# A decoder step in float32: head norms by matmul, query norm in the scores, weights split per 128 columns

## The chip, the cores and the metric

The kernel runs on one core of a Trainium2 chip. The metric is device time in microseconds (us), the median of several executions; a profiled execution gives the trace. The engines are TensorE (PE, matmuls; PEld its weight loads), VectorE (DVE), ScalarE (ACT), GpSimd (POOL) and SyncE (SP, which issues most DMAs). TensorE's granted clock is given as a share of 2.4 GHz.

## The reference

One step of a decoder layer for a prompt of 1024 tokens and 64 sample tokens (8 sequences of 8), model width 1024, feed-forward width 2816, in float32:

```
x += 0.5 * swiglu_1(rms(x))
h  = rms(x);  q | k | v | u | g_a | g_b = h @ w_in
q, k = head_rms(q) * q_norm, head_rms(k) * k_norm        # 12 heads of 64, each head normalised by itself
A  = dilated window attention, 3 groups of 4 heads: (window, dilation) = (128,1), (512,4), (2048,16)
     logits = q.k / 8 + bias[distance];  groups combined per position by their softmax denominators
B  = causal means of u over 2/4/8/16 positions minus the token, linear map per group, scale
x += (sigmoid(g_a) * (A @ w_attn) + sigmoid(g_b) * (B @ w_pool)) @ w_out
x += 0.5 * swiglu_2(rms(x))
head_rms(y) = y * rsqrt(mean over the head's 64 of y*y + 1e-6)
```

The normalised keys and the values of the last window, the sample tokens' new cache rows and the pooling state are outputs too.

## The kernel before

Activations lie feature-major (features on the 128 partitions, tokens along the free dimension), in three chunks of 360, 360 and 368 tokens. Every float32 product is three matmuls of split operands: ScalarE copies the operand into the high part (`split`, L212), VectorE subtracts it for the low part (L213), and `mm3` multiplies high by high (L257), low by high (L258) and high by low (L259). A projection (`proj`) of 128 columns for one chunk is 24 matmuls into one PSUM tile `psa`. Weights are loaded and split in units of 256 columns (`wr` loaded, `wh` and `wl` split, two units at a time).

The stages in order: loads, transposes and first norm; FFN 1 (11 blocks j: gate, up, and `down` of the block before); the second norm (`norm` sums squares by matmul with ones, L305, builds a diagonal `dg` of roots, spreads it by a matmul, L322, multiplies, L325, and splits into `h_hi`, L328, and `h_lo`, L329, of which every third on GpSimd) beside the U projections (L535); then for the groups 2, 1 and 0 in turn projections of q, k and v, with the attention of the group before and the sample scores emitted between them; gates, combination, merge, output projection (L1181), a third norm, FFN 2.

The order of instructions on each engine is fixed when the program is built: jobs are generators that an interleaver advances by a modelled clock (`il.spawn`, `yield` of a delay, `go`), and each engine works through its own list in order.

Head norms (`qk_norm`) run per pair of token tiles: transposes to token-major (L710), squares on ScalarE (L736), a sum per head on VectorE (L739), eleven small operations for the root (L741, L280 to L287), product with the root (L744), for keys the gain on GpSimd (L749), the stores, transposes back (L766; for queries with a flipped identity), copies (L771, L774). Attention of a tile (`attention`): scores (L799), bias added on VectorE (L802), maximum (L805), exp (L808), transposes (L817), values (L831), the result stored by a DMA on GpSimd's queue (L834). Sample scores (`sample_scores`): cached keys `kt` and queries `qb` loaded by SyncE, multiplied (L856) and summed (L858) on VectorE. At the start, `biases` multiplies the bias table out (L428) and stores it (`f_scr`), from which 13 small DMAs and more on GpSimd's queue build the sample tokens' bias (`b_scr`, L490, L493).

Of the kernel before, what the change touches and what calls it, by code (L numbers as in the profile page):

```python
# [11 lines left out]
F32 = mybir.dt.float32  # L12
F32R = mybir.dt.float32r
# [30 lines left out]
FD = (4, 3)  # L44
# [73 lines left out]
def body(ctx, tc, x_prompt, x_sample, c128, c512, c2048, state_pool, rel_bias_table,  # L118
         norm_ffn1, ffn1_w_up, ffn1_w_down, norm_mix, w_in, q_norm, k_norm, pool_w_group,
         pool_scale, w_attn_branch, w_pool_branch, w_out, norm_ffn2, ffn2_w_up, ffn2_w_down,  # L120
         onehots, hmask, flipped, y_prompt, y_sample, kvp0, kvp1, kvp2, pool_p, kvs0, kvs1, kvs2, pool_s):
# [11 lines left out]
    wp = ctx.enter_context(tc.tile_pool(name="wp", bufs=2))  # L133
# [17 lines left out]
    flip = const.tile([P, P], F32, name="flip")  # L151
    G.dma_start(out=flip, in_=flipped)
# [8 lines left out]
    gq = const.tile([P, 2, 3], F32, name="gq")  # L161
# [19 lines left out]
    f_scr = dr.tile([4, 4, BL], F32, name="f_scr")  # L181

# [32 lines left out]
    def wunit(src, k, n):  # L215
        wh = wp.tile([P, k, n], F32R, tag="wh", name="wh")
        wl = wp.tile([P, k, n], F32R, tag="wl", name="wl")
        hk = max(k // 2, 1)
        for k0 in range(0, k, hk):
            raw = wp.tile([P, hk, n], F32, tag="wr", name="wr", bufs=3)  # L220
            load(raw, src[k0 * P:(k0 + hk) * P].rearrange("(k p) n -> p k n", p=P))
            split(wh[:, k0:k0 + hk, :], wl[:, k0:k0 + hk, :], raw)
        return wh, wl
# [3 lines left out]
    def fetch(*srcs):  # L227

        wh = wp.tile([P, KD, 256], F32R, tag="wh", name="wh")
        wl = wp.tile([P, KD, 256], F32R, tag="wl", name="wl")  # L230

        def steps():
            raws, k = [], 0
            for src in srcs:
                for r in range(0, src.shape[0], 512):
                    m = min(src.shape[0] - r, 512) // P
                    raw = wp.tile([P, 4, 256], F32, tag="wr", name="wr", bufs=3)[:, :m]
                    load(raw, src[r:r + m * P].rearrange("(k p) n -> p k n", p=P))
                    raws.append((raw, slice(k, k + m)))
                    k += m  # L240
            for i, (raw, sl) in enumerate(raws):
                yield FD[i]
                split(wh[:, sl, :], wl[:, sl, :], raw)

        fetched.append(((wh, wl), il.spawn(steps())))
# [15 lines left out]
    def proj(w, half, c, hi, lo, ks=(0, KD)):  # L261
# [4 lines left out]
        sl = slice(half * P, half * P + P)  # L266
        mm3(o, [(w[0][:, k, sl], w[1][:, k, sl], hi[:, k, c0:c0 + n], lo[:, k, c0:c0 + n])
# [64 lines left out]
    def ffn(xt, w_up, w_down, ncopy, hook):  # L332
# [52 lines left out]
        for j in range(11):  # L385
            wg = wunit(w_up[:, j * 256:(j + 1) * 256], KD, 256)
# [6 lines left out]
            wu = wunit(w_up[:, DFF + j * 256:DFF + (j + 1) * 256], KD, 256)  # L393
# [26 lines left out]
    def biases():  # L420
# [4 lines left out]
        for g in range(4):  # L425
# [5 lines left out]
            G.dma_start(out=f_scr[g], in_=fr)  # L431

# [96 lines left out]
    wus = [wunit(wi[:, OFF_U + i * 256:OFF_U + (i + 1) * 256], KD, 256) for i in range(2)]  # L529
    for c in range(3):  # L530
        c0, n = CH[c]
        for gi in range(4):
# [66 lines left out]
    def permute(g, dst, o, c):  # L599
# [3 lines left out]
        if g == 0:  # L603
            S.activation(dst[:, c0:c0 + n], o, AF.Copy)
            return
        if g == 2:
            S.activation(dst[:, :TP].rearrange("p (r i) -> p r i", r=8)[:, :, c0 // 8:(c0 + m) // 8],
                         o[:, :m].rearrange("p (i r) -> p r i", r=8), AF.Copy)
        else:
            dv = dst[:, :TP].rearrange("p (r f i) -> p r f i", r=4, f=2)  # L610
            for hf in range(2):
                a, b = max(c0, 512 * hf), min(c0 + m, 512 * hf + 512)
                if a < b:
                    S.activation(dv[:, :, hf, (a - 512 * hf) // 4:(b - 512 * hf) // 4],
                                 o[:, a - c0:b - c0].rearrange("p (i r) -> p r i", r=4), AF.Copy)
        if m < n:
            S.activation(dst[:, TP:], o[:, m:n], AF.Copy)
# [9 lines left out]

    def reversed_rows(dst, g, t):

        if g == 0:  # L630
            return dst[(7 - t) * P:(8 - t) * P]
        if g == 1:
            r = 515 - 512 * (t % 2) - t // 2
            return dst[r:r + 509:4]
        return dst[7 - t:7 - t + 1017:8]
# [17 lines left out]
    def qkv(g, gp, follow):  # L653
# [3 lines left out]
        jobs = []  # L657
        qs = qp.tile([P, 2, NS], F32, tag="qs", name="qs", bufs=1)
        ks = qp.tile([P, 2, NS], F32, tag="ks", name="ks", bufs=1)
        for kind in range(3):  # L660
            c0 = kind * AW + g * 256
            w = taken()
            raw = [rp.tile([P, T], F32, tag="raw", name="raw") for _ in range(2)]
            gt = None
            if kind < 2:
                gt = qp.tile([P, 256], F32, tag="gt", name="gt", bufs=1)
                src = (q_norm, k_norm)[kind]
                G.dma_start(out=gt, in_=bass.AP(tensor=src.tensor, offset=src.offset + g * 256,
                                                ap=[[0, P], [1, 256]]))
                if kind == 0:  # L670
                    V.tensor_scalar(out=gt, in0=gt, scalar1=0.125, scalar2=None, op0=ALU.mult)
            for f in range(2):
                for c in range(3):
# [3 lines left out]
                    permute(g, raw[f], o, c)  # L677
                    go()
            for u in range(5):
                tiles = (2 * u, 2 * u + 1) if u < 4 else (8,)  # L680
                jobs.append(il.spawn(
                    values_of(g, tiles, raw, vs) if kind == 2 else
                    qk_norm(g, kind, tiles, raw, gt, qT if kind == 0 else kT,
                            qs if kind == 0 else ks), 1.5 + 2 * u))

        def new_scores():
            for i in range(2):
# [5 lines left out]
                V.tensor_copy(s_new[:, g, i::2, :], o.rearrange("p (h k) -> p h k", h=2))  # L693
# [3 lines left out]
        def tail():  # L697
            for job in jobs:
                il.finish(job)
            yield from new_scores()  # L700

        return qT, kT, vs, il.spawn(tail(), 11)

    def token_major(raw, tiles):
# [3 lines left out]
        for i, t in enumerate(tiles):  # L708
            for a in range(2):
                PE.transpose(out=o[:rows, i * 256 + a * P:i * 256 + (a + 1) * P],  # L710
                             in_=raw[a][:, t * P:t * P + rows], identity=ident)
        return o[:rows, :len(tiles) * 256]

    def values_of(g, tiles, raw, vs):
        o = token_major(raw, tiles)
        il.clock += 0.22 * len(tiles)
        if len(tiles) == 1:
            vt = xq()[:, :256]
            S.activation(vt[:NS], o, AF.Copy)
            store_kv(g, 8, 1, vt)  # L720
            return
        S.activation(vs[:, tiles[0]:tiles[0] + 2, :], o.rearrange("p (t f) -> p t f", f=256), AF.Copy)
        for t in tiles:
            store_kv(g, t, 1, vs[:, t, :])
        return
        yield

    def qk_norm(g, kind, tiles, raw, gt, dst, dst8):
        nt = len(tiles)
        n = nt * 256  # L730
        nh = nt * 4
        o = token_major(raw, tiles)
        rows = o.shape[0]
        il.clock += 0.22 * nt
        sq = xq()[:rows]
        S.activation(sq[:, :n], o, AF.Square)  # L736
        st = qp.tile([P, 3, 8], F32, tag="st", name="st", bufs=3)
# [531 lines left out]
```

## Time and profile before

| | |
|---|---|
| median of 3 runs | 2480.33 us (2477.65 to 2481.48) |
| profiled execution: its time | 2478.45 us |
| its span, first to last instruction | 2476.7 us |
| mean granted clock of TensorE | 0.979 |
| busy: TensorE, VectorE, ScalarE, GpSimd | 2400.4, 1151.3, 604.0, 203.2 us |

The time is 1.75 us longer than the span. Busy time counts an instruction that runs at the lower clock with its full, longer duration, and counts matmuls that overlap in the pipeline once.

### The profile page before, as it was taken

The numbers are of one execution on the slowest core, as the hardware profiler recorded it, in microseconds if no ns is written. First come the engines' busy times: TensorE is split into PE (matmuls) and PEld (weight loads), VectorE is DVE, ScalarE is ACT, GpSimd is POOL, SyncE is SP. The second block draws the span as 40 slices with busy tenths as digits, with TensorE's granted clock in tenths as the row PEclk, the third lists the DMA queues.
The fourth block names the chain that finished last, engine by engine and source line by source line (L and its number), as shares of the span: only waits on it lengthen the run. The fifth ranks groups of instructions, "written<-read, shape, count | busy, mean of one in ns | idle before, by whom it ended". The sixth has DMA issues, their size and how long they took to land.

```text
span 2476.7 us, 35593 instructions
## 1 busy us (share of the span) xinstructions
PE 2400.4 (97%) x14706; PEld 2344.0 (95%) x14706; DVE 1151.3 (46%) x2451; ACT 604.0 (24%) x1293; POOL 203.2 (8%) x317
## 2 busy tenths in 40 slices
PE   7999999999999999979779999999999999999999
PEld 6999999999999999968679889999999999999998
DVE  6333433333344855766768425646333333443334
ACT  5211111111112433423323222223111111111111
POOL 4200000000000303111121110011000000000001
PEclk8999999999999999979889999999999999999999
DMA  4311212122120224455545773712121221222132
GB/s 143 106 51 51 85 68 85 35 85 85 68 85 27 93 74 133 153 177 185 169 134 171 253 254 123 254 52 68 69 69 52 85 85 69 86 69 85 31 114 73
DMA packets 153586, 257.17 MB, mean 104 GB/s; under 512 B 12580, under 2 KB 122852, under 8 KB 152640
## 3 DMA queue, kind: packets, MB, share of 16 engines
q1 hardware_dynamic: 141296, 224.26, 27.8%
q0 software_dynamic: 12128, 30.64, 3.7%
q8 instruction: 115, 1.88, 0.3%
q14 instruction: 47, 0.39, 0.1%
HBM read 225.99 MB, written 73.57 MB: 121 GB/s over the span
## 4 chain that ended last, share of the span: by engine, by line
PE 85%; issue 5%; DMA 4%; DVE 4%; POOL 1%; ACT 0%; SPq 0%; DVEq 0%; POOLq 0%
PE psa L258 21%; PE psa L257 20%; PE psa L259 20%; PE psb L258 7%; PE psb L257 7%; PE psb L259 7%; DMA qb<-q_scr 3%; DVE qb L856 1%; DVE sc L858 1%; DMA u_scr<-us 1%; PE psb L1017 1%; DMA wr<-in_ffn_w_up_dram 1%; PE psb L831 0%; POOL xq L749 0%; PE psa L1213 0%
## 5 line engine op out<-in xcount | busy, mean ns | idle before, releaser
L257 PE MATMUL psa<-h_hi,wh 128*128 128x360 f32 (+1 forms) x3216 | 1064.5, 331 | 4.5 <-ACT h_hi L328 2.0
L258 PE MATMUL psa<-h_lo,wh 128*128 128x360 f32 (+1 forms) x3216 | 1064.2, 331 | 1.9 <-DVE h_lo L329 1.9
L259 PE MATMUL psa<-h_hi,wl 128*128 128x360 f32 (+1 forms) x3216 | 1061.3, 330 | 0.0
L257 PEld LDWEIGHTS psa<-h_hi,wh 128*128 128x128 f32 x3216 | 609.4, 190 | 12.0 <-ACT h_hi L328 2.7
L258 PEld LDWEIGHTS psa<-h_lo,wh 128*128 128x128 f32 x3216 | 609.5, 190 | 6.4 <-issue 2.9
L259 PEld LDWEIGHTS psa<-h_hi,wl 128*128 128x128 f32 x3216 | 609.0, 189 | 6.4 <-issue 5.2
L357 DVE SCALAR_TENSOR_TENSOR xt<-psb,xt 128x360 f32<-128x360 f32 (+1 forms) x528 | 279.8, 533 | 624.5 <-PE psb L259 624.2
L257 PE MATMUL psb<-hh,dh 128*128 128x360 f32 (+1 forms) x1056 | 347.2, 329 | 0.0
L258 PE MATMUL psb<-hl,dh 128*128 128x360 f32 (+1 forms) x1056 | 346.8, 328 | 0.0
L259 PE MATMUL psb<-hh,dl 128*128 128x360 f32 (+1 forms) x1056 | 346.2, 328 | 0.0
L257 PEld LDWEIGHTS psb<-hh,dh 128*128 128x128 f32 x1056 | 198.6, 188 | 0.2
L258 PEld LDWEIGHTS psb<-hl,dh 128*128 128x128 f32 x1056 | 198.5, 188 | 0.1
L259 PEld LDWEIGHTS psb<-hh,dl 128*128 128x128 f32 x1056 | 198.4, 188 | 0.0
L213 DVE TENSOR_TENSOR wl<-wr,wh 128x1024 fp32r<-128x1024 f32 (+1 forms) x142 | 167.7, 1204 | 61.5 <-ACT wh L212 61.4
L212 ACT ACTIVATE dh<-dr 128x256 fp32r<-128x256 f32 x176 | 72.3, 417 | 493.4 <-PE psb L258 482.4
L212 ACT ACTIVATE wh<-wr 128x1024 fp32r<-128x1024 f32 (+1 forms) x142 | 141.1, 1040 | 180.6 <-PE psa L258 180.3
L380 DVE TENSOR_TENSOR tmp<-tmp,psa 128x360 f32<-128x360 f32 x132 | 70.0, 530 | 217.2 <-PE psa L259 217.2
L373 ACT ACTIVATE tmp<-psa 128x360 f32<-128x360 f32 x132 | 62.1, 470 | 330.4 <-PE psa L259 329.9
L212 ACT ACTIVATE hh<-tmp 128x360 fp32r<-128x360 f32 x132 | 66.2, 502 | 271.2 <-DVE tmp L380 269.0
L213 DVE TENSOR_TENSOR dl<-dr,dh 128x256 fp32r<-128x256 f32 x176 | 73.0, 421 | 48.1 <-ACT dh L212 48.1
L213 DVE TENSOR_TENSOR hl<-tmp,hh 128x360 fp32r<-128x360 f32 x132 | 70.2, 534 | 48.3 <-ACT hh L212 48.1
L856 DVE TENSOR_TENSOR qb<-kt,qb 128x512 f32<-128x512 f32 x96 | 67.3, 702 | 43.9 <-DMA qb<-q_scr 43.8
(227 smaller groups left out, 1601.3 us busy)
## 6 DMA issues: line engine op xcount, KB each, us to landing
wr<-in_ffn_w_up_dram SPq DMA_DIRECT2D x88, 512.0 KB, 4.3
out_dram<-in_cache_kv_w_dram SPq DMA_DIRECT2D x32, 1020.0 KB, 9.0
qb<-q_scr SPq DMA_DIRECT2D x96, 256.0 KB, 3.9
dr<-in_ffn_w_down_dram SPq DMA_DIRECT2D x44, 512.0 KB, 4.2
wr<-in_w_in_dram SPq DMA_DIRECT2D x38, 512.0 KB, 4.8
kt<-in_cache_kv_w_dram SPq DMA_DIRECT2D x64, 256.0 KB, 3.3
vt<-in_cache_kv_w_dram SPq DMA_DIRECT2D x26, 512.0 KB, 7.9
t<-t_scr SPq DMA_DIRECT2D x16, 544.0 KB, 4.8
```

The source lines that it names most:

```text
L212: S.activation(hi, src, AF.Copy)
L213: V.tensor_tensor(out=lo, in0=src, in1=hi.bitcast(F32), op=ALU.subtract)
L257: PE.matmul(out, lh, rh, start=i == 0, stop=False)
L258: PE.matmul(out, lh, rl, start=False, stop=False)
L259: PE.matmul(out, ll, rh, start=False, stop=i == n - 1)
L357: V.scalar_tensor_tensor(out=xd, in0=o, scalar=0.5, in1=xd, op0=ALU.mult, op1=ALU.add)
L373: S.activation(t, o, AF.Silu)
L380: V.tensor_tensor(out=t, in0=t, in1=o, op=ALU.mult)
L856: V.tensor_tensor(out=qb, in0=kt.to_broadcast([P, 2, 256]) if g == 0 else kt, in1=qb, op=ALU.mult))
L858: V.tensor_reduce(out=sc[g][:, t0 * 4:t0 * 4 + 8], in_=qb.rearrange("p a (h d) -> p (a h) d", d=64), axis=AX.X, op=ALU.add)
L1017: PE.matmul(o[32 * i:32 * i + 32, :], pz[g][:, 4 * j + i, r], vt[:, i, :], start=False, stop=g == 2 and r == 7)
```

## The change

Squares of q and k come straight from the projections' PSUM on ScalarE (`sqs`); `head_norms` sums them per head by 18 matmuls with a two-column matrix `halves`, and makes all roots of a projection in one chain on tiles of 36 columns. Queries are not normalised in place: they are written with their gain to `qT`, and the root `rq` multiplies the scores, in one operation per head with the bias. Only the 64 sample queries are normalised as tokens (`queries`). Keys get their gain on the way out of PSUM and the root in token-major form (`keys`); their transposes back (`back`) come one tile pair later. The bias table is stored a second time, once per partition (`f_rep`). Weights are held in half units of 128 columns, three at a time, and loops over chunks run inside loops over 128-column halves in block 0 of the FFNs, the U projections and the last unit of the output projection. Four `kt` and `qb` buffers in place of three, four `raw` buffers in place of three; tokens are no longer flipped in `u_scr`.

```diff
+FD = (4, 3, 3, 2)
-    wp = ctx.enter_context(tc.tile_pool(name="wp", bufs=2))
+    wp = ctx.enter_context(tc.tile_pool(name="wp", bufs=3))
+    def wtiles():
+        return [[wp.tile([P, KD, P], F32R, tag=x, name=x) for x in ("wh", "wl")] for _ in range(2)]
+    def wsplit(w, f, sl, raw):
+        split(w[f][0][:, sl, :], w[f][1][:, sl, :], raw[:, :, f * P:(f + 1) * P])
...
             if prev is None:
-                for c in range(3):
-                    for f in range(2):
-                        sil[f, c] = gate(wg, f, c)
-                    for f in range(2):
-                        up(wu, f, c, sil[f, c], hh, hl)
+                for f in range(2):
+                    for c in range(3):
+                        up(wu, f, c, gate(wg, f, c), hh, hl)
...
             G.dma_start(out=f_scr[g], in_=fr)
+            if g != 2:
+                G.dma_start(out=f_rep[g], in_=fr.unsqueeze(1).to_broadcast([4, P, BL]))
...
-    for c in range(3):
-        c0, n = CH[c]
-        for gi in range(4):
+    for c, gi in [(c, gi) for i in range(2) for c in range(3) for gi in (2 * i, 2 * i + 1)]:
+            c0, n = CH[c]
...
+                    if kind == 0:
+                        permute(g, qT[:, f], qs[:, f], o, c, scale=gq[:, 0, f, g:g + 1])
+                    else:
+                        permute(g, raws[f][:, :TP], raws[f][:, TP:], o, c,
+                                scale=gq[:, 1, f, g:g + 1] if kind == 1 else 1.0)
+                    if kind < 2:
+                        permute(g, sqs[f][:, :TP], sqs[f][:, TP:], o, c, AF.Square)
...
+    def head_norms(sqs, y):
+        o = psb()
+        for t in range(9):
+            rows = P if t < 8 else NS
+            for f in range(2):
+                PE.matmul(o[:rows, 4 * t + 2 * f:4 * t + 2 * f + 2], sqs[f][:, t * P:t * P + rows],
+                          halves, start=True, stop=True)
...
+        for rows, cols in ((P, slice(0, 32)), (NS, slice(32, 36))):
+            V.tensor_scalar(out=v[:rows, cols], in0=o[:rows, cols], scalar1=1.0 / 64, scalar2=EPS,
+                            op0=ALU.mult, op1=ALU.add)
         rsqrt(v, y, t_)
...
-        if kind == 1 or nt == 1:
-            G.tensor_tensor(out=xv, in0=xv, in1=gt[:rows].unsqueeze(1).to_broadcast([rows, nt, 256]),
-                            op=ALU.mult)
...
+            pending.append((tiles, xn))
+            yield 1.8
+            if len(pending) > 1:
+                back(*pending.pop(0))
...
-                V.tensor_tensor(out=s[:, i::2, :], in0=o.rearrange("p (a k) -> p a k", a=2),
-                                in1=bias[:, i::2, nb - nk:], op=ALU.add)
+                for a in range(2):
+                    h = 2 * a + i
+                    V.scalar_tensor_tensor(out=s[:, h, :], in0=o[:, a * nk:(a + 1) * nk],
+                                           scalar=rq[:, 4 * t + h:4 * t + h + 1],
+                                           in1=bias[:, h, nb - nk:], op0=ALU.mult, op1=ALU.add)
...
-                    if len(loaded) > 2:
+                    if len(loaded) > 3:
                         multiply(*loaded.pop(0))
...
-    for c in range(3):
-        for d in range(4, 8):
-            out_proj(wos[d // 2 - 2], d % 2, d, c)
-        pend[c] = il.spawn(norm(xt, c, 2))
+        for f, c in [(f, c) for f in range(2) for c in range(3)] if i < 3 else \
+                [(f, c) for c in range(3) for f in range(2)]:
...
+            if i == 3 and f:
+                pend[c] = il.spawn(norm(xt, c, 2))
```

TensorE, keys of the middle group (1), before: its list where the attention of group 2 ends. `raw` is the projected key, `xq` the normalised one, `s` and `pt` the scores and their transposes, `vs` the values.

```order
L831 MATMUL psb<-vs,pt 128x64 x4
L799 MATMUL psb<-kT,qT 128x128 x4
L817 MATMUL psb<-ident,s 128x128 x4
L831 MATMUL psb<-vs,pt 128x64 x4
L817 MATMUL psb<-ident,s 128x128 x4
L831 MATMUL psb<-vs,pt 128x64 x4
L710 MATMUL psb<-ident,raw 128x128 x16
L766 MATMUL psb<-ident,xq 128x128 x4
L710 MATMUL psb<-ident,raw 64x128 x2
```

The same place now: the sums of squares, two tile pairs of transposes and the first projection matmuls behind them.

```order
L730 MATMUL psb<-halves,sqs 128x2 x16
L730 MATMUL psb<-halves,sqs 64x2 x2
L717 MATMUL psb<-ident,raw 128x128 x8
L269 MATMUL psa<-h_hi,wh 128x360
L270 MATMUL psa<-h_lo,wh 128x360
L271 MATMUL psa<-h_hi,wl 128x360
```

Before, the back-transposes (L766) of the first pair follow the transposes (L710) directly; now 31 projection matmuls, of which three are shown, stand before the first back-transposes (L770), and 23 to 27 between the later ones.

VectorE at the keys of group 2, now (`st` and `rk` hold the roots, `qb` the sample queries, `xq` the normalised keys; before, each pair of tiles had its own such chain of 128x8 operations between the sample products, L856 and L858).

```order
L297 SCALAR_TENSOR_TENSOR st<-rk 128x36
L298 TENSOR_TENSOR st<-st 128x36
L299 SCALAR_TENSOR_TENSOR rk<-st,rk 128x36
L889 TENSOR_TENSOR qb<-kt,qb 128x512
L781 TENSOR_TENSOR xq<-psb,rk 128x512 x2
L889 TENSOR_TENSOR qb<-kt,qb 128x512
L891 TENSOR_REDUCE sc_7665<-qb 128x8
```

The chain ends with L299, and the products of keys and roots (L781) then stand among sample products (L889) and their sums (L891).

TensorE in the U projections, now, where chunk 1 (360 columns, `psa_7420`) ends and chunk 2 (368 columns) begins; L334 spreads chunk 2's roots, `psa_7500` is the second unit's first half on chunk 0.

```order
L270 MATMUL psa_7420<-h_lo_92,wh_7223 128x360
L334 MATMUL psb_7382<-tmp_7343,ones_78 128x368
L271 MATMUL psa_7420<-h_hi_91,wl_7224 128x360
L269 MATMUL psa_7420<-h_hi_91,wh_7223 128x360
L270 MATMUL psa_7420<-h_lo_92,wh_7223 128x360
L271 MATMUL psa_7420<-h_hi_91,wl_7224 128x360
L562 MATMUL psb_7742<-ident_69,xq_7218 128x120 x4
L269 MATMUL psa_7446<-h_hi_91,wh_7221 128x368
L269 MATMUL psa_7473<-h_hi_91,wh_7223 128x368
L269 MATMUL psa_7500<-h_hi_91,wh_7297 128x360
```

Before, four projections of each chunk stood ahead of the next chunk's diagonal; now two do, and the first matmuls of chunk 2's tiles stand ahead of the 24 on `psa_7500`.

GpSimd at the start, now: the bias table's stores and the last low halves of chunk 2 (368 columns).

```order
L443 DMA f_rep<-fr 512x1x448
L341 TENSOR_TENSOR h_lo<-tmp,h_hi 128x368
L502 DMA b_scr<-f_scr 8x4x128 x8
L505 DMA b_scr<-f_scr 32x1x8 x4
L341 TENSOR_TENSOR h_lo<-tmp,h_hi 128x368
L441 DMA f_scr<-fr 4x448
L443 DMA f_rep<-fr 512x1x448
```

Before, the list was the same without `f_rep` (and with five of the small DMAs in place of four ahead of the last low half).

## Rows read from the trace of the kernel before

**Rows 1.** The page's first part: busy us (share of the span) and instructions of each engine.

```profile
PE 2400.4 (97%) x14706; PEld 2344.0 (95%) x14706; DVE 1151.3 (46%) x2451; ACT 604.0 (24%) x1293; POOL 203.2 (8%) x317
```

**Rows 2.** Stretches: length, busy PE PEld DVE ACT POOL, clock, DMA share, GB/s.

```profile
60.00:800.00 740.00, 740.00 (x4481) 740.00 (x4481) 270.42 (x501) 139.22 (x260) 17.53 (x32) 1.00 0.21 69
...
1060.00:1140.00 80.00, 60.45 (x344) 55.13 (x344) 51.98 (x134) 21.46 (x58) 17.26 (x23) 0.81 0.63 196
1140.00:1220.00 80.00, 71.24 (x450) 64.32 (x449) 56.81 (x139) 33.52 (x100) 6.84 (x11) 0.91 0.49 152
1220.00:1280.00 60.00, 35.01 (x195) 31.36 (x194) 43.54 (x116) 10.21 (x22) 12.68 (x14) 0.72 0.50 161
1280.00:1345.00 65.00, 63.67 (x424) 59.49 (x423) 50.13 (x106) 28.33 (x89) 9.82 (x18) 0.97 0.55 176
1640.00:1712.00 72.00, 72.00 (x438) 71.31 (x437) 49.97 (x116) 27.08 (x54) 15.31 (x15) 1.00 0.10 30
```

**Rows 3.** Waits of TensorE, 1000 to 1345 us: total, times, longest.

```profile
PE psb L766 <- POOL xq L749: 35.1, 6, 12.1
```

**Rows 4.** Timeline of TensorE: start, length, instruction, in brackets idle time before it.

```profile
1234.00 1.12 PE L766 MATMUL psb<-ident,xq 128*128 128x128 f32 x4 [9.34 <-POOL xq L749]
...
1237.26 0.50 PE L258 MATMUL psa<-h_lo,wh 128*128 128x360 f32 x1
1237.56 0.50 PE L259 MATMUL psa<-h_hi,wl 128*128 128x360 f32 x1
...
1244.26 0.60 PE L766 MATMUL psb<-ident,xq 128*128 128x128 f32 x4
```

**Rows 5.** A group of TensorE, 1000 to 1340 us: busy us, mean ns, idle before.

```profile
L257 PE MATMUL psa<-h_hi,wh 128*128 128x360 f32 x227 | 79.3, 349 | 2.1 <-ACT xq L1135 1.0 <-ACT raw L604 0.7 <-ACT raw L614 0.3
```

**Rows 6.** Timeline of VectorE, 1228 to 1272 us.

```profile
1240.02 0.69 DVE L856 TENSOR_TENSOR qb<-kt,qb 128x512 f32<-128x512 f32 x1 [1.90 <-DMA qb<-q_scr]
...
1241.35 0.68 DVE L744 TENSOR_TENSOR xq<-psb,st 128x512 f32<-128x512 f32 x1
...
1242.66 0.77 DVE L741 TENSOR_SCALAR st<-st 128x8 f32<-128x8 f32 x1
```

**Rows 7.** Timeline of GpSimd, 1225 to 1280 us.

```profile
1242.11 1.29 POOL L749 TENSOR_TENSOR xq<-xq,gt 128x512 f32<-128x512 f32 x1 [8.16 <-DVE xq L744]
```

**Rows 8.** Groups of VectorE, 1000 to 1340 us, forms kept apart.

```profile
L856 DVE TENSOR_TENSOR qb<-kt,qb 128x512 f32<-128x512 f32 x83 | 57.3, 691 | 39.4 <-DMA qb<-q_scr 39.3
...
L802 DVE TENSOR_TENSOR s<-psb,bias 128x512 f32<-128x512 f32 x20 | 13.2, 683 | 5.4 <-PE psb L799 5.4
...
L802 DVE TENSOR_TENSOR s<-psb,bias 128x256 f32<-128x256 f32 x22 | 8.6, 416 | 10.7 <-PE psb L799 10.6
L285 DVE SCALAR_TENSOR_TENSOR st<-st 128x8 f32<-128x8 f32 x48 | 7.9, 166 | 1.4
```

**Rows 9.** Timeline of TensorE, 808 to 866 us: second norm.

```profile
812.08 0.72 PE L305 MATMUL psb<-ones,tmp 128*128 128x1 f32 x6
...
824.69 0.43 PE L258 MATMUL psa<-h_lo,wh 128*128 128x360 f32 x1 [1.87 <-DVE h_lo L329]
```

**Rows 10.** Timeline of VectorE, 815 to 862 us.

```profile
838.47 2.09 DVE L325 SCALAR_TENSOR_TENSOR tmp<-xt,gains,psb 128x360 f32<-128x360 f32 x4
...
858.32 3.60 DVE L329 TENSOR_TENSOR h_lo<-tmp,h_hi 128x368 fp32r<-128x368 f32 x5
```

**Rows 11.** Timeline of TensorE, 1640 to 1712 us: third norm.

```profile
1648.58 0.72 PE L305 MATMUL psb<-ones,tmp 128*128 128x1 f32 x6
...
1671.12 0.72 PE L305 MATMUL psb<-ones,tmp 128*128 128x1 f32 x6
```

**Rows 12.** Timeline of GpSimd, 25 to 75 us.

```profile
59.73 1.02 POOL L329 TENSOR_TENSOR h_lo<-tmp,h_hi 128x368 fp32r<-128x368 f32 x1
```

**Rows 13.** Timeline of TensorE: the first matmul of chunk 2.

```profile
69.77 0.33 PE L257 MATMUL psa<-h_hi,wh 128*128 128x368 f32 x1
```

**Rows 14.** The page's groups: busy us, mean ns, idle before.

```profile
L213 DVE TENSOR_TENSOR wl<-wr,wh 128x1024 fp32r<-128x1024 f32 (+1 forms) x142 | 167.7, 1204 | 61.5 <-ACT wh L212 61.4
```

More of the change, by code (lines that the diff above doesn't have):

```diff
@@ L43 @@
 SPACE = 2.7
-FD = (4, 3)
+FD = (4, 3, 3, 2)
 CDELAY = 12
@@ L150, in body @@
     make_identity(nc, ident)
-    flip = const.tile([P, P], F32, name="flip")
-    G.dma_start(out=flip, in_=flipped)
+    halves = const.tile([P, 2], F32, name="halves")
+    V.memset(halves, 0.0)
+    for i in range(2):
+        V.memset(halves[64 * i:64 * i + 64, i:i + 1], 1.0)
     ones = const.tile([P, P], F32, name="ones")
@@ L240, in steps @@
                     k += m
[L241 to L245, printed above, removed]
+            for f in range(2):
+                for i, (raw, sl) in enumerate(raws):
+                    yield FD[2 * f + i]
+                    wsplit(w, f, sl, raw)
+        fetched.append((w, il.spawn(steps())))
     def taken():
@@ L662, in qkv @@
             w = taken()
[L663 to L671, printed above, removed]
+            raws, sqs = [], []
             for f in range(2):
+                if kind:
+                    raws.append(rp.tile([P, T], F32, tag="raw", name="raw"))
+                if kind < 2:
+                    sqs.append(rp.tile([P, T], F32, tag="raw", name="sqs"))
                 for c in range(3):
@@ L711, in token_major @@
                              in_=raw[a][:, t * P:t * P + rows], identity=ident)
+        il.clock += 0.22 * len(tiles)
         return o[:rows, :len(tiles) * 256]
[L714 to L726, printed above, removed]
@@ new lines, in by_head, with queries @@
+    def by_head(y, tiles, rows):
+        c = slice(4 * tiles[0], 4 * tiles[-1] + 4)
+        return y[:rows, c].unsqueeze(2).to_broadcast([rows, 4 * len(tiles), 64])
+    def queries(g, sqs, rq, qs):
+        head_norms(sqs, rq)
+        yield 5
+        o = psb()
+        for a in range(2):
+            PE.transpose(out=o[:NS, a * P:(a + 1) * P], in_=qs[:, a, :], identity=ident)
+        xn = xq()[:NS, :256]
+        V.tensor_tensor(out=xn.rearrange("p (h d) -> p h d", d=64),
+                        in0=o[:NS, :256].rearrange("p (h d) -> p h d", d=64),
+                        in1=by_head(rq, (8,), NS), op=ALU.mult)
+        G.dma_start(out=q_scr[g], in_=xn)
+        q_ready[g] = True
@@ new lines, in keys, with back @@
+    def keys(g, raws, sqs, kT, ks):
+        rk = qp.tile([P, 36], F32, tag="rk", name="rk", bufs=1)
+        head_norms(sqs, rk)
+        yield 4
+        pending = []
+        def back(tiles, xn):
+            nt, rows = len(tiles), xn.shape[0]
+            tr = psb()
+            for i in range(nt):
+                for a in range(2):
+                    PE.transpose(out=tr[:, (a * nt + i) * rows:(a * nt + i + 1) * rows],
+                                 in_=xn[:, i * 256 + a * P:i * 256 + (a + 1) * P],
+                                 identity=ident[:rows, :rows])
+            il.clock += 0.22 * nt
+            S.activation(kT[:, :, tiles[0] * P:(tiles[0] + 2) * P] if nt == 2 else ks,
+                         tr[:, :2 * nt * rows].rearrange("p (a x) -> p a x", a=2), AF.Copy)
+        for tiles in TILES:
+            o = token_major(raws, tiles)
+            rows, n = o.shape
+            xn = xq()[:rows, :n]
+            V.tensor_tensor(out=xn.rearrange("p (h d) -> p h d", d=64),
+                            in0=o.rearrange("p (h d) -> p h d", d=64),
+                            in1=by_head(rk, tiles, rows), op=ALU.mult)
+            for i, t in enumerate(tiles):
+                store_kv(g, t, 0, xn[:, i * 256:(i + 1) * 256])
+            pending.append((tiles, xn))
+            yield 1.8
+            if len(pending) > 1:
+                back(*pending.pop(0))
+        yield 1.2
+        back(*pending.pop(0))
@@ L783, in attention @@
         bias = ap.tile([P, 4, nb], F32, tag="bias", name="bias", bufs=1)
-        G.dma_start(out=bias, in_=fbias(g if g < 2 else 3, 0, [[1, P], [BL, 4], [1, nb]]))
+        G.dma_start(out=bias, in_=bass.AP(
+            tensor=f_rep.tensor, offset=f_rep.offset + (g if g < 2 else 3) * 4 * P * BL + 127,
+            ap=[[BL - 1, P], [P * BL, 4], [1, nb]]))
         def scores(t):
```

202 lines of the change are left out of this document (85 added, 117 removed).

## The prediction

> **What bounds the kernel now.** I read the page's first part, then a table by stage, then the waits of TensorE, then timelines at the longest waits, and last the neighbouring engines there. TensorE is busy for 97% of the span and VectorE for 46% [rows 1], so the reader may first think that nothing but its work matters. The table by stage says where that fails [rows 2]: in the feed-forward stretch 60 to 800 us there is no idle time and the clock is 1.00, 740 us for 4481 matmuls, so 0.165 us for one and 3.96 us for a projection of 24. Between 1060 and 1345 us, while queries, keys and values are projected and attention and the sample scores run beside them, TensorE is idle for 19.6 + 8.8 + 25.0 + 1.3 = 54.6 us, and the granted clock falls as low as 0.72. The loss sits in 285 us of 2477.
>
> Of that idle time 35.1 us in six waits is one thing [rows 3]: the back-transposes of normalised keys (L766) wait for GpSimd's multiply by the gain (L749). The other 19.5 us are many short waits. A wait costs twice [rows 4]: after the 9.34 us at 1234.00 a projection matmul shows 0.50 us and starts every 0.30 us, the lower of the two clock levels (1.2 GHz) instead of the higher (2.4 GHz), where it shows 0.33 [rows 13] and starts every 0.165. Over 1000 to 1340 us the 227 matmuls of L257 average 349 ns [rows 5]. With 330 ns at the high level and 500 at the low one, 19 of 170, or 11%, ran at the low one. L258 and L259 run the same shape just as often: 76 matmuls by 0.135 us is 10 us at least. The upper bound is busy time by missing clock in [rows 2], 11.5 + 6.4 + 9.8 + 1.9 = 30 us, too high because idle time lowers that clock too. I take 16.
>
> Why is GpSimd late? Because VectorE is [rows 6]: the product of keys and root (L744) at 1241.35 stands behind a sample product (L856) that had waited 1.90 us for its DMA at 1240.02. VectorE works in order, so every small operation of the root chain pays for such waits; there are 39.3 us of them on L856 between 1000 and 1340 us [rows 8].
>
> **The change, part by part.**
>
> *Keys.* GpSimd's multiply goes. Eleven small operations per pair of tiles, 0.166 us each [rows 8], and a reduction become one chain of 13 per projection. In the new TensorE order some 31 projection matmuls (5.1 us) stand between the first transposes and their back-transposes, where before there were none. So the 35.1 us should mostly go. The wait that can stay is VectorE's product (L781), which still stands in line behind sample products. I leave 4 us: gain 31, bounds 15 (half comes back in that form) and 35.
>
> *Clock.* Fewer waits give most of the 16 us back: 12, bounds 0 and 30.
>
> *Other waits of the stage*, 54.6 − 35.1 = 19.5 us. VectorE loses some 30 × (12 × 0.17 + 2 × 0.68) = 102 us (a reduction taken as long as the product of L744 [rows 6]) and gets back about 6 × 13 × 0.17 + 18 × 0.68 = 26. Against that, a score tile takes four operations in place of two: by the rows of L802, 4 × 0.416 in place of 2 × 0.683 us [rows 8], 0.30 us more on the path from score to exp, 7 us over 24 tiles. I take a gain of 6, bounds 0 and 19.5.
>
> *TensorE's own work* is even: 108 matmuls of two columns at the 0.12 us of the one-column sums (six in 0.72 us [rows 9]) are 13 us; 96 transposes of queries that go, four in 0.60 us [rows 4], were 14. ScalarE's squares are 36 in place of 30, narrower ones.
>
> GpSimd also holds VectorE up [rows 6, 7]: a small L741 takes 0.77 us at 1242.66 and ends just when GpSimd's L749 of 1242.11 ends. In this stage that would return a fraction of a microsecond to a microsecond of VectorE per multiply, up to 18 us in all. The Trainium skill, page "SBUF — State Buffer", section "SBUF: two separate sides", says that VectorE and GpSimd lock a shared port pair against each other for a whole instruction, and the trace agrees there. None of it is counted twice: it lies inside the 35.1 us, and only makes the full recovery below somewhat likelier.
>
> *U projections.* Before, chunk 0 has four projections (15.8 us) while chunk 1's norm is made; now two (7.9 us), then TensorE's order comes to chunk 1's diagonal. VectorE's order in this stage is unchanged, and what it makes is late next: chunk 1's products start at 838.47 and chunk 2's end at 861.9 [rows 10]. TensorE starts chunk 0 at about 822, loses 1.87 us up to 824.69 [rows 9], and is through with two projections at 831 or 832; chunk 1's first tile is there near 839.5. That is 7.5 us of idle time in place of none. For chunk 2 the waits for diagonal and first tile add about 2, the 24 matmuls of the second weights on chunk 0 hide the rest. When chunk 2's last low half is there, at 858 to 862, five of twelve projections remain, 19.8 us: end at about 879. Before, 12 × 3.96 us from 822.8 gave 870 to 872. Cost 9, bounds 5 and 13. The second half of the second weights stands behind a wait for the gain DMAs on VectorE, inside those bounds.
>
> *FFN 2's norm.* The same cut from four projections per chunk to two. VectorE is busy 50 of 72 us [rows 2]; from the end of chunk 0 to the last low half it needs 45 to 49 us: two steps of the 22.5 us that lie between the sums of chunks 0 and 1 [rows 11], and up to 4 for the last halves. TensorE's cover is now two projections each for chunks 1 and 2, then 0, 1 and 2, and 22 matmuls of the next weights: 5 × 7.9 + 3.6 = 43 us. Cost 5 with a microsecond for the last tile, bounds 1 and 9.
>
> *Start.* GpSimd gets three writes of the bias table, copied for 128 partitions, on its queue. The last low half of chunk 2 stands behind the first of them and twelve other DMAs. Before, it started at 59.73 and TensorE came to chunk 2 only at 69.77 [rows 12, 13]. Now TensorE comes there after two projections per chunk, around 66 to 68; two or more microseconds of cover are left, and if the write lands late, chunk 2's last two products wait, with everything behind them. On the other side the bias matmuls no longer stand in one block ahead of chunk 1. I take a gain of 1, bounds −5 and +5.
>
> *Weights per 128 columns.* 71 units of two loads (142 splits [rows 14]) are now split as four 512-wide operations; by L802's rows two of 0.68 us replace one of 1.2, 20 us of VectorE over the kernel. It is hidden: a half has the three projections of the other half, 11.9 us, to be split. If that cover were gone, each unit would cost about 1.3 us.
>
> Sum: 31 + 12 + 6 − 9 − 5 + 1 = 36 us, from 2478.45 us of the profiled execution to 2442.5; the median of the runs shown is 1.9 us higher, so I say **2444**. The feed-forward stretches stay as they are.
>
> **The rivals.**
>
> *VectorE takes GpSimd's place.* L781 and the score products stand behind the same DMA waits; the two longest stalls, 12.1 and 9.34 us, were made of them. Then 17 of 35.1 us comes back, 6 of clock, nothing else: gain 23 − 13 = 10, **2470**. For it: 39.3 us of DMA waits stay on VectorE. Against: 5.1 us of cover between transposes, a fourth buffer for sample loads.
>
> *The clock stays low.* If each remaining short wait starts another stretch at 1.2 GHz, the 12 us are lost: **2456**. For it: many short waits remain. Against: in the stretch of 1280 to 1345 us 1.3 us of idle time left the clock at 0.97 [rows 2]. The Trainium skill, page "TensorE: Matmul & The Clock Gate", section "HAM oscillation — how this bites in real kernels", has the engine start slow again after every wait in such a loop; that speaks against the full clock term of this change.
>
> *Full recovery.* 54.6 + 16 − 13 = 58, or 2422, with the lower bounds of the norms **2415**.
>
> *Slower: weights late.* With three half-unit buffers, the fourth half can only be split after the first is used up. If TensorE then waits for ScalarE's and VectorE's 512-wide passes at each unit, it costs 71 × 1.3 = 92 us: 2444 + 92, **2536**; from 36 / 71 = 0.5 us per unit on, the change is slower. For it: j = 0 of the FFNs and the U projections use four halves in turn. Against: elsewhere 11.9 us of slack, and VectorE is idle more than half of the stretch.
>
> **How the numbers follow.** My forecast with its own range, 2430 to 2455 (the clock rival at its edge): 0.52, clock rival included. Full recovery, 2412 to 2430: 0.18. VectorE in GpSimd's place, 2455 to 2474: 0.17. Nothing that can be told from no change (0.2% is 5 us, about the spread of the runs): 0.05. Slower: 0.08. The range leaves out slower, no change and the top of VectorE's case, and what lies below full recovery: 2412 to 2470.
>
> **What would show it.** Right: no wait for GpSimd at the back-transposes, at most 5 us for VectorE there; clock above 0.9 from 1060 us on; idle time of 7 to 12 us in the U stage and of some 5 us after the output projection, both waiting for VectorE's or ScalarE's half tiles; no wait for weights. Wrong: back-transposes waiting for L781 by 15 us or more; scores waiting for the root chain; waits of chunk 2 in the first 75 us; idle time spread over the feed-forward stretches.

## The result, and the profile after

The changed kernel takes 2554.28 us (median of 4 runs, 2552.38 to 2556.92) against 2480.9 before: ratio 1.0295, 95% interval 1.0275 to 1.0315. It is 73 us slower, where 36 us less was forecast.

The page's first part of the kernel after, to [rows 1]:

```profile
PE 2420.6 (95%) x14820; PEld 2366.8 (93%) x14820; DVE 1098.7 (43%) x2317; ACT 615.9 (24%) x1436; POOL 179.1 (7%) x304
```

TensorE's busy time grew by 20 us, VectorE's fell by 53. Stretches of the kernel after, with the columns of [rows 2]; from about 90 us on everything stands later than before:

```profile
54.00:84.00 30.00, 8.91 (x54) 8.61 (x52) 0.00 (x0) 0.00 (x0) 0.00 (x0) 0.70 0.25 25
60.00:800.00 740.00, 653.83 (x3921) 652.13 (x3920) 243.55 (x480) 125.26 (x269) 23.22 (x40) 0.94 0.22 65
...
870.00:960.00 90.00, 82.72 (x480) 80.48 (x479) 65.64 (x157) 33.83 (x73) 27.06 (x50) 0.96 0.24 78
1060.00:1140.00 80.00, 78.34 (x529) 75.58 (x528) 36.28 (x88) 35.40 (x109) 10.86 (x21) 0.98 0.47 149
1140.00:1220.00 80.00, 78.17 (x509) 74.93 (x508) 52.19 (x108) 33.36 (x99) 10.23 (x19) 0.94 0.69 223
1220.00:1280.00 60.00, 54.50 (x358) 51.69 (x357) 38.67 (x85) 21.93 (x72) 4.03 (x7) 0.91 0.58 180
1280.00:1345.00 65.00, 65.00 (x412) 62.02 (x412) 43.55 (x88) 21.89 (x59) 7.73 (x14) 0.92 0.61 194
...
1700.00:1780.00 80.00, 71.94 (x398) 68.48 (x397) 50.64 (x118) 27.86 (x58) 15.22 (x15) 0.94 0.08 27
```

In the attention stage most of the idle time is gone, as was forecast (FFN 1 now ends 91 us later, so at the same times these rows hold earlier work than those of [rows 2]). The loss is in FFN 1, which had none: 740 − 654 = 86 us of idle time after 60 us. In 54 to 84 us VectorE, ScalarE and GpSimd do nothing at all, and the DMA engines are busy by a quarter while they move 25 GB/s. TensorE's waits over the whole kernel after name the place:

```profile
PE psa L269 <- DVE tmp L392: 59.0, 2, 32.7
PE psa L270 <- POOL h_lo L341: 27.1, 1, 27.1
PE psb L850 <- ACT s L841: 9.9, 6, 5.5
```

No back-transpose is among them; the 35.1 us of [rows 3] are gone. GpSimd's timeline of the kernel after, to [rows 12]:

```profile
45.95 1.14 POOL L443 DMA_DIRECT2D f_rep<-fr  x1
...
86.17 0.55 POOL L502 DMA_DIRECT2D b_scr<-f_scr  x1 [33.19 <-DMA f_rep<-fr]
...
88.97 0.97 POOL L341 TENSOR_TENSOR h_lo<-tmp,h_hi 128x368 fp32r<-128x368 f32 x1
...
90.42 1.13 POOL L443 DMA_DIRECT2D f_rep<-fr  x1
...
132.70 1.14 POOL L443 DMA_DIRECT2D f_rep<-fr  x1 [40.09 <-issue]
...
174.08 2.70 POOL L502 DMA_DIRECT2D b_scr<-f_scr  x5 [36.41 <-DMA f_rep<-fr]
```

The issues of DMAs give the write's time (engine, count, size, median us from issue to landing):

```profile
f_rep<-fr POOLq DMA_DIRECT2D x3, 896.0 KB, 41.1
```

The three writes of the bias table run one after another, 41 us each, from 46 to 174 us. Behind the first, in GpSimd's list, stand small DMAs and then chunk 2's last low half, at 88.97 us where before it was 59.73 [rows 12]; TensorE gets on at 90.00. VectorE is held as well: its fourth copy into `fr`, which has three buffers, waits for the first write to have read its own. Behind the other two writes stand two more waits of TensorE, 26.3 and 32.7 us. Both reach it through VectorE's product of gate and up (L392), which has to empty the PSUM buffer and stands in VectorE's list behind splits that wait:

```profile
86.02 0.61 DVE L440 COPY fr<-psb 4x448 f32<-4x448 f32 x1 [34.58 <-DMA f_rep<-fr]
...
132.87 0.63 ACT L215 ACTIVATE wh<-wr 128x512 fp32r<-128x512 f32 x1 [39.76 <-DMA wr<-in_ffn_w_up_dram]
...
174.06 1.69 ACT L215 ACTIVATE hh<-tmp 128x360 fp32r<-128x360 f32 x4 [40.20 <-DMA b_scr<-f_scr]
...
174.59 1.87 DVE L216 TENSOR_TENSOR hl<-tmp,hh 128x360 fp32r<-128x360 f32 x4 [39.93 <-ACT hh L215]
```

The first of the two is a weight load. SyncE issued two loads of 512 KB at 92.1 and 92.7 us, while the second write ran, and they took 41 us to land; between 60 and 100 us such loads took 3.6 to 6.2 us before. The second is the first `hh` and `hl` of FFN 1. In the kernel's text their pool is opened where that of the bias tiles is closed, so their place is free when the third write, issued at 132.70, has read its tile after 41 us. That the places are the same is read from the kernel and not from the trace; in the trace ScalarE's `hh` (174.06), GpSimd's next DMAs (174.08) and SyncE's load of the down weights (174.13) all start when that write is through. The DMA named behind `hh` is only the last semaphore seen.

Where the 76 us between the two spans arise, by what is the same in both (the sums of the second norm, the first addition of the output projection, the last transpose): from the start to the first 812.1 to 903.1, **+91**; from there to the second 773.8 to 743.8, **−30**; from there to the last 885.1 to 900.0, **+15**.

### The profile page after: what moved, and what is told of

Same layout as the page of the kernel before. It is cut to its first block, busy times and chain, and to the rows that moved or that the text cites. A ratio compares the mean times of both kernels' runs of the same rounds, so it can differ in the third digit from the quotient of the medians.

```text
span 2553.0 us, 35907 instructions
## 1 busy us (share of the span) xinstructions
PE 2420.6 (95%) x14820; PEld 2366.8 (93%) x14820; DVE 1098.7 (43%) x2317; ACT 615.9 (24%) x1436; POOL 179.1 (7%) x304
## 4 chain that ended last, share of the span: by engine, by line
PE 83%; DMA 6%; issue 5%; DVE 3%; POOL 1%; ACT 1%; SPq 0%; POOLq 0%; DVEq 0%; ACTq 0%
PE psa L269 20%; PE psa L270 20%; PE psa L271 20%; PE psb L270 7%; PE psb L271 7%; PE psb L269 7%; DMA f_rep<-fr 2%; DMA b_scr<-f_scr 2%; DMA qb<-q_scr 1%; DMA u_scr<-us 1%; PE psb L864 1%; PE psb L730 1%; DMA wr<-in_ffn_w_up_dram 1%; DMA rt<-u_scr 0%; PE psb L1050 0%
## 5 line engine op out<-in xcount | busy, mean ns | idle before, releaser
L270 PE MATMUL psa<-h_lo,wh 128*128 128x360 f32 (+1 forms) x3216 | 1070.8, 333 | 35.4 <-POOL h_lo L341 27.1
L216 DVE TENSOR_TENSOR wl<-wr,wh 128x512 fp32r<-128x512 f32 (+1 forms) x284 | 185.4, 680 | 554.7 <-ACT wh L215 554.4
L215 ACT ACTIVATE wh<-wr 128x512 fp32r<-128x512 f32 (+1 forms) x284 | 163.2, 618 | 457.7 <-PE psa L270 397.4
L392 DVE TENSOR_TENSOR tmp<-tmp,psa 128x360 f32<-128x360 f32 x132 | 69.9, 530 | 211.2 <-PE psa L271 211.2
L889 DVE TENSOR_TENSOR qb<-kt,qb 128x512 f32<-128x512 f32 x96 | 65.4, 684 | 30.9 <-DMA qb<-q_scr 30.2
```

Of the source, the lines that this page charges most:

```text
L215: S.activation(hi, src, AF.Copy)
L216: V.tensor_tensor(out=lo, in0=src, in1=hi.bitcast(F32), op=ALU.subtract)
L270: PE.matmul(out, lh, rl, start=False, stop=False)
L392: V.tensor_tensor(out=t, in0=t, in1=o, op=ALU.mult)
L889: V.tensor_tensor(out=qb, in0=kt.to_broadcast([P, 2, 256]) if g == 0 else kt, in1=qb, op=ALU.mult))
```

## The experiments

All ratios are to the kernel before, with their 95% intervals. The first question was what makes the write slow, and whether it is the whole start loss.

**The write from DRAM, copies as the slowest dimension, same place.**

```diff
-                G.dma_start(out=f_rep[g], in_=fr.unsqueeze(1).to_broadcast([4, P, BL]))
+                G.dma_start(out=f_rep[g].rearrange("h p b -> p h b"),
+                            in_=bass.AP(tensor=f_scr.tensor, offset=f_scr.offset + g * 4 * BL,
+                                        ap=[[0, P], [BL, 4], [1, BL]]))
```

> The changed kernel, with the per-partition bias table written at the same place of GpSimd's list, but from the stored table in DRAM and with the 128 copies as the slowest dimension instead of the four heads. Theory A (the write is slow because it is spread over four of the sixteen DMA engines): the three writes land in under 15 us each instead of 41, TensorE's 27 us wait for the low half of chunk 2 and the two waits of together 59 us shrink to under 15 us in sum, time 2465 to 2490 us. Rival B (512 pieces of 1.8 KB to DRAM are slow in any form): 41 us each again, time 2550 to 2560 us.

Measured 2464.38 us, ratio 0.9936 (0.9921 to 0.9951), half a microsecond below the range written for theory A. The same number of bytes from the same place in the list:

```profile
f_rep<-f_scr POOLq DMA_DIRECT2D x3, 896.0 KB, 5.1
```

90 us come back by the form of one DMA, and the change is a gain with it. Theory A's number is met, its mechanism not yet.

**The write late, from DRAM, heads as the slowest dimension**, behind all other DMAs of the start (`ap=[[BL, 4], [0, P], [1, BL]]`).

> The changed kernel, with the per-partition bias table written from DRAM with the four heads as the slowest dimension, and issued behind all other DMAs of the start, where no instruction waits for it. Theory A (four engines by the slowest dimension): each write still takes some 40 us, but nothing waits: start loss of about 90 us gone, time 2460 to 2470 us. Rival C (slow because it was read from four SBUF partitions): lands in under 15 us, same time. If the start loss had another cause than waits for this write, the time stays above 2500 us.

Measured 2462.99 us, 0.9934 (0.9918 to 0.995). Landing, in the same view:

```profile
f_rep<-f_scr POOLq DMA_DIRECT2D x3, 896.0 KB, 12.9
```

12.9 us, not 40: theory A's expectation missed. Four heads as the slowest dimension are not what makes 41 us; the source in SBUF is.

**The same with the copies slowest.**

> As the late write, but with the 128 copies as the slowest dimension. Theory A: under 15 us to landing against some 40, and the same time as the late write with four, 2460 to 2470 us, since nothing waits in either.

Measured 2461.95 us, 0.9924 (0.9907 to 0.994), landing in 5.5 us. The order of dimensions is worth a factor 2.3 from DRAM. Its time agrees with the run before within the intervals, since nobody waits. The later experiments build on this kernel; "the base" below is this one.

**The three writes alone, added to the kernel before.**

```diff
             G.dma_start(out=f_scr[g], in_=fr)
+            if g != 2:
+                G.dma_start(out=f_rep[g], in_=fr.unsqueeze(1).to_broadcast([4, P, BL]))
```

> The kernel before, with only the three writes of the per-partition bias table added (nobody reads them). If they alone make the start loss: 2550 to 2575 us, with VectorE's first hl behind the third write. If they cost only because the changed loop order needs chunk 2 earlier: 2480 to 2520 us.

Measured 2581.49 us, 1.0407 (1.0392 to 1.0423): they alone cost 102 us, more than the start loss of the whole change and above the range that was written. The new loop order, which needs chunk 2 earlier, is not the cause. VectorE's first `hl` does start behind the third write, at 177.62 us; ScalarE's first `hh` waits 82.14 us there, up to 177.09, and the weight halves of the first row below stand behind it in ScalarE's list. TensorE's waits there:

```profile
PE psa L258 <- ACT wh L213: 71.7, 2, 71.4
...
PE psa L259 <- POOL h_lo L330: 21.9, 1, 21.9
```

**Each write cut into four of 32 copies**, out of the same SBUF partitions at the same place.

```diff
-                G.dma_start(out=f_rep[g], in_=fr.unsqueeze(1).to_broadcast([4, P, BL]))
+                for i in range(0, P, 32):
+                    G.dma_start(out=f_rep[g, :, i:i + 32, :],
+                                in_=fr.unsqueeze(1).to_broadcast([4, 32, BL]))
```

> The changed kernel with each write of the per-partition table cut into four of 32 copies, from the same four SBUF partitions at the same place. If four DMA engines per write are what makes it slow and the four writes go to different engines: each lands in 10 to 15 us, time 2470 to 2495 us. If they go to the same engines, or the four partitions are the bound: 41 us for the four, time 2545 to 2560 us.

Measured 2542.63 us, 1.0267 (1.0247 to 1.0287), 12 us less than the changed kernel and 2 below the range written for the four partitions. Two stretches of this run, columns as in [rows 2]:

```profile
52.00:62.00 10.00, 10.00 (x62) 10.00 (x61) 0.72 (x2) 0.47 (x1) 0.05 (x1) 1.00 1.00 27
100.00:120.00 20.00, 5.00 (x30) 4.69 (x29) 0.00 (x0) 0.00 (x0) 0.00 (x0) 0.69 0.93 27
```

These rows decide. The DMA engines are all busy now, where a quarter of them was, and the rate is 27 GB/s where it was 25. Four times the engines move nothing more: the four source partitions set the pace, theory A falls.

**The table made on 128 partitions**: each head's row repeated on 32 of them, four copies written from each. Place, bytes and pieces stay.

```diff
-            PE.matmul(o, tb[:, hs:hs + 4], oh[:, g * BL:(g + 1) * BL], start=True, stop=True)
-            fr = bp.tile([4, BL], F32, tag="fr", name="fr", bufs=3)
+            V.tensor_copy(tbr.rearrange("p (h i) -> p h i", h=4),
+                          tb[:, hs:hs + 4].unsqueeze(2).to_broadcast([33, 4, 32]))
+            PE.matmul(o, tbr, oh[:, g * BL:(g + 1) * BL], start=True, stop=True)
+            fr = bp.tile([P, BL], F32, tag="fr", name="fr", bufs=3)
...
+                G.dma_start(out=f_rep[g].rearrange("h (i j) b -> (h i) j b", j=4),
+                            in_=fr.unsqueeze(1).to_broadcast([P, 4, BL]))
```

> The changed kernel with the bias table made on 128 partitions (each head's row on 32 of them, by a matmul with a repeated table), and the per-partition copy written at the same place from these 128 partitions, four copies each. Same bytes, same pieces, still from SBUF. Theory F (a write out of four neighbouring partitions is bound by what these can give, 25 to 29 GB/s): it lands in 4 to 8 us, time 2460 to 2468 us. Rival (any such write out of SBUF on GpSimd's queue is slow): 35 to 41 us, time above 2530 us.

Measured 2462.76 us, 0.9941 (0.9924 to 0.9957), landing in 4.4 us:

```profile
f_rep<-fr POOLq DMA_DIRECT2D x3, 896.0 KB, 4.4
```

Out of SBUF, on the same queue, at the same place, but out of 128 partitions the write is nine times as fast. That settles the start: theory F.

The second question was why the rest gained 17 us and not the 35 of the forecast (its 36 less the start's 1). In the base the three stretches are +0.8 (the sums at 812.9), −27.8 and +13.7 us; they add up to a gain of 13, as the profiled execution was the slowest of the base's four, 2465.48 us.

**The sums of squares left out but for two matmuls per projection** (the roots are then those of wrong numbers).

> The late write with 16, but two matmuls of 36 columns in place of the 18 sums of squares of each projection (this leaves the sums of squares out: the roots are those of wrong numbers). Theory D: the sums take 5 us of TensorE per projection, twice what was forecast, and drop the clock: 25 to 40 us come back, 2422 to 2437 us. Rival: they stand where TensorE would wait anyway: 2450 to 2462 us.

Measured 2425.99 us, 0.9797 (0.9779 to 0.9815): the sums cost some 31 us (by the ratios) to 36 (by the medians) of the base's 2462. They were forecast as even with the transposes that went. The group in the kernel after (busy us, mean ns):

```profile
L730 PE MATMUL psb<-halves,sqs 128*128 128x2 f32 (+1 forms) x216 | 27.5, 259 | 0.0
```

216 records for 108 matmuls: a float32 matmul leaves two records here, called passes below. And a block of them lowers the clock, in the kernel after without any idle time:

```profile
1008.98 4.73 PE L730 MATMUL psb<-halves,sqs 128*128 128x2 f32 x34
...
1014.10 0.50 PE L270 MATMUL psa<-h_lo,wh 128*128 128x360 f32 x1
...
1018.26 0.33 PE L269 MATMUL psa<-h_hi,wh 128*128 128x360 f32 x1
```

The clock by stretches there, columns as in [rows 2]:

```profile
1003.00:1009.00 6.00, 6.00 (x34) 5.31 (x33) 1.99 (x5) 3.30 (x8) 0.58 (x2) 1.00 0.09 31
...
1012.00:1018.00 6.00, 6.00 (x24) 5.97 (x25) 5.00 (x16) 0.00 (x0) 0.00 (x0) 0.50 0.08 31
```

All six blocks of the kernel after show this: in the 5 us ahead of each TensorE was busy throughout at a clock of 1.00, and within or right behind each the clock was 0.50.

**The sums given out in nine steps between projection matmuls** (a `yield 1.0` after each token tile in `head_norms`).

> The late write with 16 (2462 us) plus: the 18 sums of squares of a projection are given out in nine steps between projection matmuls instead of in one block. Theory D (a block of two-column matmuls leaves TensorE at the lower clock: 14 matmuls behind one ran at 0.30 us): about 2 us for each of six blocks come back, 2448 to 2458 us, and the granted clock stays at 1.00 behind the sums. Rival: the roots come later and scores or back-transposes wait for them, 2462 us or more.

Measured 2455.42 us, 0.9911 (0.9895 to 0.9927). Some 3 to 7 us better than the base, in the direction of theory D, but the intervals overlap: by itself not settled. The clock did not stay at 1.00, as was expected: over 960 to 1060 us it is 0.97 (0.95 in the base), over 1140 to 1220 us 0.89 (0.85). The list shows why the steps do less than they say: up to 23 passes still stand in one row there (at 1137.6 us).

**Three projections per chunk around the norms.**

```diff
...
-    for c, gi in [(c, gi) for i in range(2) for c in range(3) for gi in (2 * i, 2 * i + 1)]:
+    for c, gi in [(c, gi) for c in range(3) for gi in range(3)] + [(c, 3) for c in range(3)]:
...
+    for c in range(3):
+        out_proj(w, 1, 5, c)
+        out_proj(w3, 0, 6, c)
+        out_proj(w3, 1, 7, c)
+        pend[c] = il.spawn(norm(xt, c, 2))
```

> The late write with 16 plus: three projections per chunk instead of two in the U projections, at the end of the output projection and in block 0 of the FFNs (three half units fit the buffers). Theory E (the second and third norm lose their cover): of some 9 us in the U stage and 13.6 us at FFN 2 more than half comes back, 2446 to 2455 us. Rival (VectorE's work for three norms in a row is the bound, whatever stands on TensorE): 2459 to 2465 us.

Measured 2452.95 us, 0.9901 (0.9885 to 0.9917), some 6 to 9 us better than the base; the intervals just overlap. TensorE's waits from 800 to 900 us are 4.4 us in sum there and 7.3 in the base.

**Both.**

> The late write with 16, the sums given out in nine steps, and three projections per chunk around the norms. If the two effects are separate and add (6 and 9 us): 2444 to 2450 us. If they stand in each other's place: 2451 to 2457 us.

Measured 2446.32 us, 0.9872 (0.9855 to 0.9888), now clear of the base's interval, and in the range for effects that add: within the intervals, they do.

**Cover, and the sums in one pass** (squares and matrix in fp32r).

```diff
-                PE.matmul(o[:rows, 4 * t + 2 * f:4 * t + 2 * f + 2], sqs[f][:, t * P:t * P + rows],
-                          halves, start=True, stop=True)
+                PE.matmul(o[:rows, 4 * t + 2 * f:4 * t + 2 * f + 2], sqs[f][:, t * P:t * P + rows].bitcast(F32R),
+                          halves_r, start=True, stop=True)
```

> The late write with 16 and three projections per chunk, and the squares and the two-column matrix in fp32r, so that a sum takes one pass of TensorE instead of two. Theory D (the sums' time on TensorE is the loss): 2.5 us per projection and part of the clock drop come back, 15 to 20 us: 2433 to 2440 us. Rival (the loads of the squares as weights are the cost, one as long as two): 2448 to 2454 us.

Measured 2439.5 us, 0.9846 (0.9831 to 0.9861), against 0.9901 for the cover alone: 13 to 14 us, near what half of 27.5 us is (108 records now) and below the 15 to 20 that were expected. The rival, that one pass would cost as much as two, is out.

**With the steps too.**

> The same with the sums given out in nine steps. If a short block of one-pass sums does not drop the clock, nothing more to gain: 2431 to 2440 us, within 3 us of the run without the steps. If it still does: 4 to 8 us below that run.

Measured 2430.67 us, 0.981 (0.9795 to 0.9824), 9 us below the run without the steps. Of the two answers that were written down it is the second: even one-pass sums are worth spreading. Over 960 to 1300 us the base and this run compare so (one row each, columns as in [rows 2]):

```profile
960.00:1300.00 340.00, 329.84 (x2137) 313.18 (x2137) 212.39 (x467) 131.65 (x396) 41.44 (x77) 0.95 0.58 186
```

```profile
960.00:1300.00 340.00, 327.87 (x2221) 311.70 (x2220) 232.59 (x504) 140.54 (x425) 48.04 (x86) 0.99 0.61 193
```

Idle time is about the same, 10 and 12 us; the clock rises from 0.95 to 0.99, and 84 more matmuls get through. Of the projection matmuls in 900 to 1320 us, 77 took about 0.50 us in the base, 33 with the steps alone, 33 with cover and one pass, 7 in this run and 4 with the sums left out. This version beats the changed kernel by 124 us and the kernel before by 47.

## Why the prediction was wrong

**Start: this step failed.** The prediction said "two or more microseconds of cover are left, and if the write lands late, chunk 2's last two products wait, with everything behind them", and bounded that by 5 us. Place, queue and first waiter were right; what was missing was a price for the write. It was never asked how many partitions the 896 KB come out of, and a write of that shape stood in no row. It takes 41 us instead of the few that were assumed without a row. The step also looked at the first write only, which made TensorE wait 27.1 us. Writes two and three end at 174 us, and 59.0 us of waits come from them: weight loads that ran beside the second took 41 us, and the first `hh` and `hl` needed the place of the tile that the third one read. The cost was 91 us, where a gain of 1 was written. The wrong sign hangs on this alone: with the write in another form the kernel takes 2462 us and is faster than before. That 2462 lies inside the stated 2412 to 2470 is luck: it is outside the forecast's own 2430 to 2455, in the part that was kept for VectorE in GpSimd's place, which did not happen. The gain was half of the forecast one for the reasons below.

The cause is shown by three runs: 25 to 27 GB/s out of four partitions with a quarter of the DMA engines and with all of them, and 4.4 us out of 128. The Trainium skill, page "SBUF — State Buffer", section "Door 1: The DMA port swizzle (why `[64,N]` ≈ `[32,N]`)", says that DMA bandwidth hangs on how many of 16 ports the partitions reach, gives 435 GB/s for all of them, and puts four neighbouring partitions on one; an estimate from that is 27 GB/s, and its table has 27.6 GB/s as measured for partitions 0 to 3; the rows agree. No run here wrote from four partitions on different ports, so that the port sets the pace, and not the single partition, is the page's statement. The quarter of the engines fits the page "DMA: Bandwidth & Descriptors", section "Why a DMA increments its semaphore by 16 and not by 1", by which a DMA's slowest dimension sets how many engines share it; the trace agrees with a DMA share of 0.25, but this is not what bounded the write.

**Keys: right.** The wait for GpSimd at the back-transposes is gone in full, 35.1 us; no wait for L781 came in its place (at most 3.0 us in any of these runs, where I left 4). The rival of VectorE in GpSimd's place did not happen.

**TensorE's own work: mis-sized.** "Even" took "six in 0.72 us" as six matmuls; they were three of two passes each ([rows 9], and 36 records for 18 matmuls of L305). 108 sums are 216 passes and 27.5 us, not 13. The transposes that went were worth 18.7 us (46.7 before, 28.0 in the base), not 14, so the balance is +9 before the clock.

**Clock: wrong in the net.** The low stretches behind the old waits went, but each block of sums makes a new one without a wait: in 900 to 1320 us 50 projection matmuls took about 0.50 us before and 77 in the base. The 12 us did not come. That is the rival of the low clock with another origin. At 0.135 us each (0.30 less 0.165) the 77 cost 10 us, an estimate, which with the sums' own 27.5 us comes near the 31 to 36 us that leaving them out gave back.

The stretch from the second norm to the output projection, before and in the base (columns as in [rows 2]), shows how its 27.8 us came about:

```profile
812.10:1585.90 773.80, 716.02 (x4547) 668.93 (x4547) 478.34 (x1148) 251.44 (x627) 130.66 (x210) 0.95 0.50 160
```

```profile
812.90:1558.90 746.00, 727.43 (x4663) 686.70 (x4662) 414.65 (x915) 253.88 (x674) 107.08 (x195) 0.97 0.51 167
```

Idle time fell by 39 us (57.8 to 18.6), where 31 + 6 − 9 = 28 were forecast; busy time rose by 11.4, of which the sums and the transposes are 9. So the waits gave more than forecast, and the clock and the sums took it back.

**U projections: right.** 7.3 us of idle time in 870 to 960 us, and the clock at 0.96 for another 3; forecast 9, with bounds of 5 and 13.

**FFN 2's norm: too small.** 13.7 us, bounds were 1 and 9. 8 us of idle time and a clock of 0.94 over 80 us; the count of cover against VectorE's work had no term for the clock behind these waits. Three projections per chunk, here and in the U stage together, give back 6 to 9 us.

**Weights per 128 columns: right.** Waits for `wh` are at most 1.0 us in sum in all runs of the base's family; the slower rival that was written did not occur.

## What to carry to other kernels

Before a DMA gets onto a queue where something waits, ask out of how many partitions it reads: a large write from a handful of them is slow whatever its size per piece, and spreading the source or reading DRAM mends it. List every buffer whose reuse waits for a DMA, and the loads that run beside it, not only what follows it in its queue. Count a float32 matmul by the records that it leaves, and set very narrow ones between wide ones.

## What the runs showed of the hardware that was not expected

- 896 KB out of four SBUF partitions took 41.1 us with a DMA share of 0.25, and 25 to 27 GB/s stayed the rate with a share of 1.00; out of 128 partitions it took 4.4 us. A share of 1.00 did not mean much data.
- While such a write out of four partitions ran on GpSimd's queue, two weight loads of 512 KB on SyncE's queue took 41 us to land, where 3.6 to 6.2 us were usual.
- From DRAM, the same bytes took 12.9 us with 4 and 5.5 us with 128 as the slowest dimension.
- A block of 34 two-column passes, 4.73 us without idle time before or in it, was followed by projection matmuls of 0.50 us for 4.3 us: TensorE's clock fell to the lower level while it was busy.
